# A hybrid encoder layer: order of the in-projection's column groups, who sums and splits x, and what is kept of the weights in DRAM

## The chip, the cores and the metric

The kernel runs on one core of a Trainium2 chip. The core has a matrix engine (TensorE, PE in the profile), a vector engine (VectorE, DVE), a scalar engine (ScalarE, ACT), GpSimd (POOL) and a sync engine (SyncE, SP) that here only issues DMAs; ScalarE and GpSimd can issue DMAs too. Each engine works through its own instructions in order, and semaphores join the engines. The time is microseconds on the device, the median of three runs.

## What is computed

One layer of a streaming encoder, float32, width 1024, for 2048 tokens of a prompt and 8x16 tokens of a decode batch (together 17 tiles of 128 tokens, the last one the decode batch's). In short:

```python
z = x @ w_in                      # 1024 -> 2824 columns
mq, mk, mv, og, li, lf, q, k, v = split_in(z)      # mLSTM: 4 x 512; gates 4 + 4
mlstm = mlstm_chunkwise(mq, mk, mv, li, logsigmoid(lf), C0, n0, m0)   # chunks of 64
attn = band_attend(rope(q), rope(k), v, sinks)     # 8 query, 2 key heads of 64
mix = concat(head_norm(mlstm) * sigmoid(og), attn) @ w_out
x = layer_norm(alpha * x + mix)
up = causal_conv(x @ w_up)                         # 1024 -> 2 x 2816, width 3
x = layer_norm(alpha * x + (silu(gate) * value) @ w_down)
```

The new states, caches and the last rows of the up-projection are outputs as well.

## The kernel before

**Float32 products.** A float32 matrix is split into two fp32r halves: ScalarE copies it to the high half (L205 for weights, L535 for x), VectorE subtracts that to get the low half (L206, L536). A product is then three matmuls: high by high, high by low, low by high.

**Winograd blocks.** The in-projection works on 2x2 blocks with seven products instead of eight, named 1 to 7 (a Strassen-Winograd scheme). Products 1, 2 and 4 use plain blocks of the weights, products 6, 5, 7 and 3 (`SUMS`) use sums of them; likewise with x. The sums of x are t1 to t4 in `x_steps` (L505), made in place in the raw blocks of x by VectorE, which then splits them. For the later token blocks, the low halves of x of products 2, 4 and 5 (b and s in the code at L536) are made by GpSimd, and so are the rope's last adds (L843).

**Tiling.** Four token blocks (`IBLOCKS`) of four tiles, the first with the decode tile besides. For each block five weight groups of 512 columns: two of mLSTM queries and keys, then the mLSTM values (group 2), the output gate (group 3) and the attention's queries (group 4, whose eviction `i_out` at L726 runs through the rope). Each group has seven products of 24 matmuls (`i_product`, L667) that add into three PSUM banks; `i_after` evicts them, on ScalarE and VectorE (L737 to L749). Behind the last products of a block come its direct tiles ("t", `i_direct`, L693): 264 columns of gate logits, attention keys and values, 24 matmuls a tile, in two banks by turns. `i_keys` (L697) evicts them: ScalarE copies gates and values, VectorE makes the rope of the keys (L838, L841, L842), GpSimd adds its two parts (L843), SyncE stores. Then the next block's products 1, 7, 6 and 2 follow.

**The passage.** While a block's last group runs, the next block's x is loaded and its sums and splits are made (`passage`, in `i_dense`): loading behind product 7, then steps 7, 3, b12, t1, t2 behind products 5, 3 and 4, then 1, 6, 2, 5, t4 behind the second direct tile.

**Weights.** `next_raw` (L397) loads 512 KB blocks into raw slots, `next_split` (L436) splits them into a ring of halves, as soon as TensorE has released some. In block 0 `split_first` (L464) makes the sums of the weights from the plain blocks and stores them raw into `zws` in DRAM (L471); the later blocks load the plain blocks from `wi` and the sums from `zws`, and split both again. `d_sums` puts sums of the down-projection's weights into the first groups. The queue of SyncE carries all these transfers in order, and the stores of every output too.

**What is around it.** From block 1 on, the mLSTM and attention work of earlier tiles ("chains") is woven into TensorE's order: that order is written out, the other engines' order comes from the program's order and the scheduler. `logs_of` (gate logarithms of a block) and `i_done` set when a block's chains may begin. The out-projection follows at about 790 us with the rest of the attention, then LayerNorm, then from about 1060 us the feed-forward part: its first block of tokens (`FBLOCKS`) loads six tiles of h from `zh` (L1570), transposes them on TensorE (L1579) and splits them.

## Time and profile before

| | |
|---|---|
| Median of 3 runs | 2517.73 us (2516.81 to 2523.47) |
| Profiled execution | 2523.84 us |
| its span | 2522.1 us |
| mean granted TensorE clock | 0.97 |
| In-projection with its chains | 0 to some 790 us |
| Out-projection | 790 to 1050 us |
| Feed-forward | 1060 us to the end |
| DMA | 600.07 MB, mean 238 GB/s |

How to read the profile's lines: a group of instructions has line, engine, operation, output<-input by the program's names, count, then busy us, the mean of one in ns, the idle time of the engine just before them and what ended most of it. Names: `wraw` raw weights, `w` their halves, `xr` raw x, `oh` and `ol` the halves of x, `dps` the PSUM banks, `u`, `zev` evicted products, `kve` keys and values, `rb` the second part of a rope, `zws` the stored sums of weights, `hst` rows of h. `PE ... <- DVE ...` in a list of waits is TensorE held by VectorE: us in total, how often, the longest. A row of the timeline has start, duration, engine, line, instruction, and in brackets the idle time before it and what ended it. `SPq` is SyncE's queue.

### The profile page before, as it was taken

The numbers are of one execution on the slowest core, as the hardware profiler recorded it, in microseconds if no ns is written. First come the engines' busy times: TensorE is split into PE (matmuls) and PEld (weight loads), VectorE is DVE, ScalarE is ACT, GpSimd is POOL, SyncE is SP. The second block draws the span as 40 slices with busy tenths as digits, with TensorE's granted clock in tenths as the row PEclk, the third lists the DMA queues.
The fourth block names the chain that finished last, engine by engine and source line by source line (L and its number), as shares of the span: only waits on it lengthen the run. The fifth ranks groups of instructions, "written<-read, shape, count | busy, mean of one in ns | idle before, by whom it ended". The sixth has DMA issues, their size and how long they took to land.

```text
span 2522.1 us, 39870 instructions
## 1 busy us (share of the span) xinstructions
PE 2378.4 (94%) x14425; PEld 2176.6 (86%) x14425; DVE 1898.1 (75%) x3221; ACT 1271.8 (50%) x2286; POOL 404.7 (16%) x395
## 2 busy tenths in 40 slices
PE   8989978998997899799999999999999999999998
PEld 7979877987886777589999999999999988778776
DVE  7688497778757776598778877677766678796897
ACT  4444455665564553265555655555545454444453
POOL 0031041223112424310000000001100000220300
PEclk9999989999998999899999999999999999999999
DMA  7858647656756535568776788986998876756652
GB/s 276 296 196 313 215 157 249 220 172 227 240 179 222 187 128 177 203 223 321 291 269 267 255 308 314 314 301 233 316 307 266 263 268 202 245 184 194 219 191 108
DMA packets 290021, 600.07 MB, mean 238 GB/s; under 512 B 46108, under 2 KB 139296, under 8 KB 289824
## 3 DMA queue, kind: packets, MB, share of 16 engines
q1 hardware_dynamic: 288096, 591.23, 68.6%
q0 software_dynamic: 1728, 6.29, 0.7%
q8 instruction: 114, 1.87, 0.3%
q14 instruction: 83, 0.68, 0.1%
HBM read 433.17 MB, written 164.26 MB: 237 GB/s over the span
## 4 chain that ended last, share of the span: by engine, by line
PE 49%; DVE 11%; DMA 4%; issue 4%; ACT 4%; POOL 1%; SPq 0%; DVEq 0%; ACTq 0%; POOLq 0%
PE dps L1714 13%; PE fup L1714 13%; PE fht L1917 5%; PE dps L1917 5%; PE fup L1917 4%; DMA zf<-cc 2%; DVE cc L1762 2%; PE dps L667 2%; PE dps L210 2%; PE dps L211 1%; PE dps L212 1%; ACT cc L1760 1%; DVE uw L206 1%; DVE w L206 1%; ACT sc L1239 1%
## 5 line engine op out<-in xcount | busy, mean ns | idle before, releaser
L1714 PE MATMUL dps<-hh,uw 128*128 128x384 f32 (+1 forms) x1848 | 481.7, 329 | 6.8 <-ACT u L1739 1.9
L1714 PE MATMUL fup<-hh,uw 128*128 128x384 f32 (+1 forms) x1848 | 480.8, 328 | 2.9 <-ACT u L1739 2.3
L1714 PEld LDWEIGHTS dps<-hh,uw 128*128 128x128 f32 x1848 | 330.1, 188 | 10.7 <-ACT u L1739 3.1
L206 DVE TENSOR_TENSOR w<-wraw,w 128x1024 fp32r<-128x1024 f32 (+2 forms) x203 | 262.5, 1301 | 97.3 <-ACT w L205 93.5
L1714 PEld LDWEIGHTS fup<-hh,uw 128*128 128x128 f32 x1848 | 330.3, 188 | 4.8 <-ACT u L1739 3.9
L1762 DVE SCALAR_TENSOR_TENSOR cc<-u,cw,cc 128x768 f32<-128x768 f32 (+1 forms) x264 | 252.4, 977 | 108.7 <-ACT cc L1760 106.9
L205 ACT CAST w<-wraw 128x1024 fp32r<-128x1024 f32 (+2 forms) x203 | 200.5, 995 | 211.9 <-PE dps L667 97.1
L1714 PE MATMUL fup<-hl,uw 128*128 128x384 f32 (+1 forms) x924 | 302.9, 328 | 0.7 <-DVE hl L206 0.7
L1714 PE MATMUL dps<-hl,uw 128*128 128x384 f32 (+1 forms) x924 | 302.5, 327 | 0.0
L667 PE MATMUL dps<-w,oh 128*128 128x256 f32 x1344 | 266.1, 291 | 11.1 <-ACT zev L743 4.4
L667 PEld LDWEIGHTS dps<-w,oh 128*128 128x128 f32 x1344 | 219.0, 195 | 24.1 <-issue 9.2
L205 ACT CAST uw<-wraw 128x1024 fp32r<-128x1024 f32 x126 | 123.0, 978 | 203.8 <-PE dps L1917 94.0
L206 DVE TENSOR_TENSOR uw<-wraw,uw 128x1024 fp32r<-128x1024 f32 x126 | 150.6, 1197 | 61.4 <-ACT uw L205 61.2
L667 PE MATMUL dps<-oh,w 128*128 128x256 f32 x896 | 175.6, 290 | 18.3 <-DVE zev L747 8.7
L667 PE MATMUL dps<-w,ol 128*128 128x256 f32 x672 | 192.1, 286 | 0.0
L1760 ACT ACTIVATE cc<-u,cw 128x768 f32<-128x768 f32 (+1 forms) x132 | 129.6, 998 | 122.1 <-DVE u L1753 60.7
L1917 PE MATMUL fup<-uw,fu 128*128 128x512 f32 x726 | 177.9, 401 | 8.1 <-DVE yacc L1946 4.5
L1917 PEld LDWEIGHTS fup<-uw,fu 128*128 128x128 f32 x726 | 138.2, 191 | 43.5 <-DVE yacc L1946 5.4
L1714 PEld LDWEIGHTS fup<-hl,uw 128*128 128x128 f32 x924 | 173.5, 188 | 1.4 <-DVE hl L206 1.4
L1714 PEld LDWEIGHTS dps<-hl,uw 128*128 128x128 f32 x924 | 173.5, 188 | 0.0
L667 PEld LDWEIGHTS dps<-oh,w 128*128 128x128 f32 x896 | 144.8, 194 | 30.0 <-DVE zev L747 9.8
L1917 PE MATMUL dps<-uw,fu 128*128 128x512 f32 x660 | 164.6, 395 | 0.0
(343 smaller groups left out, 4855.2 us busy)
## 6 DMA issues: line engine op xcount, KB each, us to landing
uw<-zw SPq DMA_DIRECT2D x176, 512.0 KB, 4.7
zw<-uw SPq DMA_DIRECT2D x88, 512.0 KB, 2.9
wv<-wup SPq DMA_DIRECT2D x66, 512.0 KB, 5.3
wraw<-wi SPq DMA_DIRECT2D x65, 512.0 KB, 4.6
wraw<-zws SPq DMA_DIRECT2D x60, 512.0 KB, 3.9
wraw<-zt SPq DMA_DIRECT2D x60, 512.0 KB, 4.2
wraw<-wdn SPq DMA_DIRECT2D x45, 512.0 KB, 4.1
wraw<-wo SPq DMA_DIRECT2D x40, 512.0 KB, 4.4
```

Source lines behind the costliest of these rows:

```text
L205: nc.scalar.copy(hi, src)
L206: nc.vector.tensor_sub(lo, src, hi.bitcast(F32))
L210: mm(out, ah, bh, start=start, stop=False)
L211: mm(out, ah, bl, start=False, stop=False)
L212: mm(out, al, bh, start=False, stop=stop)
L667: mm(o, l, r, start=s in (1, 7) and c == k == i == 0, stop=k == 3 and i == 2, skip_group_check=True)
L1239: nc.scalar.activation(sc[:, j, :N], sc[:, j, :N], AF.Exp, bias=mx[:, j:j + 1], scale=0.125, accum_out=sm[:, j:j + 1])
L1714: mm(ps, l[:, k], r[:, k], start=s in (1, 7) and k == 0 and i == 0, stop=k == 3 and i == 2, skip_group_check=True)
L1760: S.activation(c[:, v], u[:, v, 2:2 + n], AF.Identity, bias=w[3], scale=w[2])
L1762: V.scalar_tensor_tensor(c[:, v], u[:, v, i:i + n], w[i], c[:, v], op0=ALU.mult, op1=ALU.add)
L1917: mm(ps, l[:, k, c], r[:, k], start=s in (1, 4, 7) and u == 0 and k == 0 and i == 0, stop=u == nu - 1 and k == n - 1 and i == 2, skip_grou ...
```

## The change

- The attention's queries are weight group 2 and the mLSTM values group 4; the output gate stays group 3. The last group before the direct tiles so has no rope, and its outputs go to `zv`.
- The sums of x: t3 is made in a buffer of its own (`xt`, a raw slot), t2 adds to it there, t4 goes to the fourth raw block and t1 to the second. The steps are spread over the last group: loading behind product 1, t3 and 7 behind 7, t2 and 6 behind 6, 3 and t4 behind 3, b12 and t1 behind 4; 1 and 2 behind the second direct tile; 4 and 5 behind the fourth. All low halves of x are made by VectorE.
- The rope gets the engine of its last add: VectorE for keys, GpSimd for queries as before.
- Sums of weights of groups 2, 3 and 4 (`KEPT = 2`) are stored into `zws` as two halves after the split in block 0, and in blocks 1 to 3 both halves are loaded straight into the ring of halves: 36 units, with no raw slot and no split. Groups 0 and 1 work as before.
- `logs_of` of a block is called three items (products or tiles) after its second direct tile instead of right behind it, and its chains may begin one item later than before.
- The six tiles of h of the feed-forward's first block are loaded by ScalarE's queue instead of SyncE's.

The diff, with the definition of constants, array allocations and the decode tile's stores cut:

```diff
+KEPT = 2
@@ -95,7 +97,7 @@
     w = f("w_in")[0]
     qa = w[:, 2056:2568].reshape(D, 2, 4, 64).transpose(0, 2, 1, 3).reshape(D, 512)
     qk = [np.concatenate([w[:, c:c + HT], w[:, 512 + c:512 + c + HT]], 1) for c in (0, HT)]
-    wi = np.stack([*qk, w[:, 1024:1536], w[:, 1536:2048], qa], 0)
+    wi = np.stack([*qk, qa, w[:, 1536:2048], w[:, 1024:1536]], 0)
 
     a["wi"] = wi.reshape(NG, 2, 4, P, 2, HT).transpose(0, 4, 1, 3, 2, 5)
     w4 = np.concatenate([w[:, 2052:2056], w[:, 2048:2052], w[:, 2568:2824]], 1)
...
@@ -394,6 +396,10 @@
         while self.next_split() or self.next_raw():
             pass
 
+    def kept(self, u):
+
+        return u[0] == "p" and u[1] > 0 and u[2] >= KEPT and u[3] in SUMS
+
     def next_raw(self):
         nc, a = self.nc, self.a
         if self.ur >= len(self.uq):
@@ -401,7 +407,7 @@
         u = self.uq[self.ur]
 
         there = u[0] == "p" and u[1] == 0 and (u[2] == 0 and u[3] != 1 or u[3] in (5, 4, 3) or u[2:] == (1, 1))
-        if not there and not self.raw_free():
+        if not there and not self.kept(u) and not self.raw_free():
             return False
         self.ur += 1
         if u[0] == "p":
@@ -421,9 +427,11 @@
                     return True
                 self.raw_of[g, quad[s]] = e = self.raw_slot([P, 4, HT])
                 src = a["wi"][g][quad[s]]
+            elif self.kept(u):
+                return True
             else:
                 self.raw_of[u] = e = self.raw_slot([P, 4, HT])
-                src = a["wi"][g][quad[s]] if s in (1, 2, 4) else self.zws[g][SUMS.index(s)]
+                src = a["wi"][g][quad[s]] if s in (1, 2, 4) else self.zws[g][SUMS.index(s)][0]
             nc.sync.dma_start(e[0], src)
         elif u[0] == "g":
             self.raw_of[u] = e = self.raw_slot([P, 2, 264])
@@ -450,7 +458,10 @@
             self.wu[u] = w[:, 0], w[:, 1]
             return True
         hi, lo = self.half([P, 1024]), self.half([P, 1024])
-        if u[0] == "p" and u[1] == 0:
+        if self.kept(u):
+            for i, t in enumerate((hi, lo)):
+                self.nc.sync.dma_start(t.bitcast(F32), self.zws[u[2]][SUMS.index(u[3])][i].rearrange("p a b -> p (a b)"))
+        elif u[0] == "p" and u[1] == 0:
             self.split_first(u[2], u[3], hi, lo)
         else:
             e = self.raw_of.pop(u)
@@ -468,7 +479,8 @@
         a11, a12, a21, a22 = (0, 0), (0, 1), (1, 0), (1, 1)
 
         def keep(q, m):
-            nc.sync.dma_start(self.zws[g][SUMS.index(m)], r[q])
+            if g < KEPT:
+                nc.sync.dma_start(self.zws[g][SUMS.index(m)][0], r[q])
         if s == 7:
             V.tensor_sub(r[a11], r[a11], r[a21])
             keep(a11, 7)
@@ -483,6 +495,9 @@
         for i in range(n):
             c = slice(i * 1024 // n, (i + 1) * 1024 // n)
             self.split(hi[:, c], lo[:, c], f[:, c])
+        if g >= KEPT and s in SUMS:
+            for i, t in enumerate((hi, lo)):
+                nc.sync.dma_start(self.zws[g][SUMS.index(s)][i].rearrange("p a b -> p (a b)"), t.bitcast(F32))
         if s == (6 if g == 0 else 2):
             V.tensor_sub(r[a12], r[a12], r[a11])
             keep(a12, 3)
@@ -505,35 +520,30 @@
 
         nc, V = self.nc, self.nc.vector
         r = lambda q: self.xr[b, q]
-
-        src = {1: 1, 2: 3, 3: 4, "b12": 2, 5: 2, 6: 4, 4: 1}
-        if b == 0:
-            src = {1: 1, 2: 3, 3: 4, "b12": 2, 5: 1, 7: 2, 6: 4, 4: 3}
         for s in steps:
-            if s == "t1":
-                V.tensor_sub(r(src[5]), r(2), r(1))
+            if s == "t3":
+                self.spare = False
+                self.xt = e = self.raw_slot([P, 4, HT]) if b else [self.tp.tile([P, 4, HT], F32, name="xt", tag="qk", bufs=2), False]
+                V.tensor_sub(e[0], r(4), r(2))
             elif s == "t2":
-                V.tensor_sub(r(4), r(4), r(src[5]))
+
+                V.tensor_add(self.xt[0], self.xt[0], r(1))
             elif s == "t4":
-                V.tensor_sub(r(src[4]), r(3), r(4))
-            elif s == "t3":
-                V.tensor_sub(r(2), r(4), r(2))
+
+                V.tensor_sub(r(4), r(3), self.xt[0])
+                self.xt[1] = True
+            elif s == "t1":
+
+                V.tensor_sub(r(2), r(2), r(1))
             else:
-                if s == 7 and b:
-                    e = self.raw_slot([P, 4, HT])
-                    self.spare = False
-                    V.tensor_sub(e[0], r(4), r(2))
-                    e[1] = True
-                    x = e[0]
-                else:
-                    x = r(src[s])
+                x = self.xt[0] if s in (7, 6) else r({1: 1, 2: 3, 3: 4, "b12": 2, 5: 2, 4: 4}[s])
 
                 self.hx[b, s] = h, l = self.x_slot(4 if s == "b12" else s)
                 n = 4 if (b, s) == (0, "b12") else 1
                 for i in range(n):
                     k = slice(i * 4 // n, (i + 1) * 4 // n)
                     nc.scalar.copy(h[:, k], x[:, k])
-                    (nc.gpsimd if b and s in (2, 4, 5) else V).tensor_sub(l[:, k], x[:, k], h[:, k].bitcast(F32))
+                    V.tensor_sub(l[:, k], x[:, k], h[:, k].bitcast(F32))
 
     def x_single(self, *steps):
 
@@ -580,18 +590,20 @@
         self.x_load(0, 3)
         self.x_steps(0, 1)
         self.advance()
-        self.x_steps(0, 2, "t1", "t3", 7, "t2", 6)
+        self.x_steps(0, 2, "t3", 7, "t2", 6)
         self.x_single(4)
-        self.x_steps(0, 5, "t4")
+        self.x_steps(0, "t1", 5, "t4")
         self.sb, self.trans = {}, None
 
-        passage = {7: ["load"], 5: [7], 3: [3], 4: ["b12", "t1", "t2"]}
+        passage = {1: ["load"], 7: ["t3", 7], 6: ["t2", 6], 3: [3, "t4"], 4: ["b12", "t1"]}
         sums = 0
         after = None
         for item in self.items:
             if after:
 
                 after[0] -= 1
+                if after[0] == 1:
+                    self.logs_of(after[1] - 1)
                 if after[0] < 0:
                     self.i_done = after[1]
                     after = None
@@ -607,14 +619,15 @@
                 self.i_keys(b, ti, ps)
                 if ti == 1:
                     if b + 1 < nb:
-                        self.x_steps(b + 1, 1, 6, 2, 5, "t4")
+                        self.x_steps(b + 1, 1, 2)
                     else:
                         self.release(4)
-                    self.logs_of(b)
-                    after = [3, b + 1]
+                    after = [4, b + 1]
                 elif ti == 3 and b or ti == 4:
                     self.release(4)
                     self.x_steps(b, 4)
+                    if b:
+                        self.x_steps(b, 5)
                 self.advance()
                 continue
             _, b, g, s = item
@@ -650,6 +663,7 @@
                 if s == 3:
                     sums += 1
         assert sums == NK2
+        self.logs_of(nb - 1)
         self.chains.hold = False
 
     def i_product(self, b, g, s):
@@ -700,7 +714,7 @@
         nc.scalar.copy(self.gates[b][:, ti, :], ps[:, :8])
         kv = self.mp.tile([P, 2 * P], F32, name="kve", tag="kve", bufs=2)
         nc.scalar.copy(kv[:, P:], ps[:, 136:264])
-        self.rope(ps[:, 8:136], kv[:, :P], t, 1)
+        self.rope(ps[:, 8:136], kv[:, :P], t, 1, nc.vector)
         nc.sync.dma_start(self.zkv[t], kv)
 
     def i_store(self, b, g, i, j, ev):
@@ -711,7 +725,7 @@
             f = 4 * i + 2 * g
             nc.sync.dma_start(self.zqk[b][f:f + 2, :, j * HT:(j + 1) * HT].rearrange("f p m -> p f m"), v)
         else:
-            z = (self.zv, self.zog, self.zqa)[g - 2]
+            z = (self.zqa, self.zog, self.zv)[g - 2]
             for c in range(2):
                 nc.sync.dma_start(z[IBLOCKS[b][2 * j + c]][:, i * HT:(i + 1) * HT], v[:, c])
 
@@ -724,9 +738,9 @@
     def i_out(self, b, g, i, j, src):
 
         nc = self.nc
-        if g == 4:
+        if g == 2:
             A = self.zev()
-            self.rope(src, A, IBLOCKS[b][2 * j], 2)
+            self.rope(src, A, IBLOCKS[b][2 * j], 2, nc.gpsimd)
             self.i_store(b, g, i, j, A)
             return
         ev = src if i else self.zev()
...
@@ -827,7 +841,7 @@
         nc.sync.dma_start(self.zt[0, k], x)
         nc.sync.dma_start(self.zt[1, k], y)
 
-    def rope(self, src, A, t, nt):
+    def rope(self, src, A, t, nt, adder):
 
         V = self.nc.vector
         n = src.shape[-1]
@@ -840,7 +854,7 @@
         over = lambda z: z.to_broadcast([P, nt, n // (64 * nt), 32])
         V.tensor_mul(h(B, 0), h(src, 1), over(ms))
         V.tensor_mul(h(B, 1), h(src, 0), over(sin))
-        self.nc.gpsimd.tensor_add(A, A, B)
+        adder.tensor_add(A, A, B)
 
     def rope_load(self, t, nt):
 
@@ -1567,7 +1581,7 @@
             if ti < len(tiles):
                 tag = tags[ti] if ti < len(tags) else "hst"
                 hs[ti] = fp.tile([P, D], F32, name="hst", tag=tag, bufs=2 if tag == "hst" else 1)
-                nc.sync.dma_start(hs[ti], self.zh[tiles[ti]])
+                (nc.sync if b else nc.scalar).dma_start(hs[ti], self.zh[tiles[ti]])
 
         for ti in range(len(tags)):
             load(ti)
```

More of the change, by code (lines that the diff above doesn't have):

```diff
@@ L289, in setup @@
         self.zqk = [dp.tile([8, P, P * len(b)], F32, name=f"zqk{i}") for i, b in enumerate(IBLOCKS)]
-        self.zws = [[dp.tile([P, 4, HT], F32, name=f"zws{g}_{i}") for i in range(4)] for g in range(NG)]
+        self.zws = [[dp.tile([1 if g < KEPT else 2, P, 4, HT], F32, name=f"zws{g}_{i}") for i in range(4)] for g in range(NG)]
         self.zv = [dp.tile([P, 512], F32, name=f"zv{t}") for t in range(NT)]
@@ L777, in i_batch @@
         t = NPT
-        if g == 4:
+        if g == 2:
             A = self.zev()
-            self.rope(ps, A, t, 1)
+            self.rope(ps, A, t, 1, nc.gpsimd)
             nc.sync.dma_start(self.zqa[t], A)
@@ L793, in i_batch @@
             nc.scalar.copy(ev, ps)
-        nc.sync.dma_start((self.zv, self.zog)[g - 2][t], ev)
+        nc.sync.dma_start((self.zog, self.zv)[g - 3][t], ev)
     def i_transposes(self):
```

## The prediction

> **What bounds the kernel now.** I read the page first, then the span cut into stretches of 100 us, then TensorE's waits, whole and by stretch, and last the timeline where these waits fall.
>
> ```profile
> span 2522.1 us, 39870 instructions
> PE 2378.4 (94%) x14425; PEld 2176.6 (86%) x14425; DVE 1898.1 (75%) x3221; ACT 1271.8 (50%) x2286; POOL 404.7 (16%) x395
> ```
>
> TensorE is the bound, busy for 94% of the span. So the change, which leaves its matmuls as they are, can only take away its gaps and the slow clock behind them. In the stretches the columns are the window, its length, each engine's busy time (with its number of records), the granted clock, the DMA share and GB/s:
>
> ```profile
> 200.00:300.00 100.00, 98.09 (x795) 91.83 (x794) 63.00 (x110) 41.09 (x75) 12.84 (x10) 0.95 0.82 281
> 300.00:400.00 100.00, 80.81 (x617) 74.98 (x615) 83.11 (x210) 51.69 (x128) 31.94 (x21) 0.91 0.56 179
> ```
>
> The first lies inside token block 1 and has almost no gap. The second holds the change of blocks (I call it a passage: the last product of a block, four direct tiles of keys, values and gates at L693, the first products of the next), and 19 us are missing. VectorE, 63 us in the first, has 83 in the second, with more GpSimd beside it. The waits of TensorE over the in-projection say who ends the gaps (us in total, times, longest), and the same question put to the three passages (140 to 215, 335 to 400, 565 to 610 us) and to 1000 to 1120 us gives the second fence:
>
> ```profile
> PE dps L693 <- DVE rb L842: 25.2, 4, 12.1
> PE pq L1185 <- DMA qa<-zqa: 10.2, 1, 10.2
> ...
> PE dps L667 <- DVE zev L747: 8.7, 5, 2.8
> ```
>
> ```profile
> PE dps L693 <- DVE rb L842: 8.6, 1, 8.6
> ...
> PE dps L693 <- DVE rb L842: 12.1, 1, 12.1
> PE ppt L1252 <- DVE C L1173: 3.6, 1, 3.6
> ...
> PE dps L693 <- DVE rb L842: 4.5, 2, 2.7
> PE dps L693 <- DVE u L749: 4.2, 1, 4.2
> ...
> PE fht L1579 <- DMA hst<-zh: 15.3, 1, 15.3
> ```
>
> L842 is the last VectorE instruction of the rope (rotary embedding) on a direct tile's keys: it gives the PSUM bank back, and the third tile needs the first tile's bank. So VectorE's queue in the passage is the bound. The timeline of passage 2 shows what stands in it:
>
> ```profile
> 348.65 0.40 PE L693 MATMUL dps<-w,oh 128*128 128x264 f32 x2
> ...
> 348.85 0.69 DVE L749 TENSOR_TENSOR u<-dps,u 128x512 f32<-128x512 f32 x1 [1.05 <-PE dps L667]
> ...
> 354.37 0.28 PE L693 MATMUL dps<-w,ol 128*128 128x264 f32 x1
> ...
> 359.47 3.35 POOL L536 TENSOR_TENSOR ol<-xr,oh 128x1024 fp32r<-128x1024 f32 x1 [2.26 <-ACT oh L535]
> 360.56 3.36 DVE L206 TENSOR_TENSOR w<-wraw,w 128x1024 fp32r<-128x1024 f32 x1
> 363.84 1.21 DVE L514 TENSOR_TENSOR xr<-xr 128x1024 f32<-128x1024 f32 x1
> ...
> 366.44 0.21 DVE L842 TENSOR_TENSOR rb<-dps,ropet 128x64 f32<-128x64 f32 x1
> ...
> 366.79 0.78 PE L693 MATMUL dps<-w,oh 128*128 128x264 f32 x2 [12.14 <-DVE rb L842]
> ```
>
> From the last product's eviction (348.85) to the rope's end, VectorE works for 17.8 us without a stop, where TensorE has two tiles, 6.0 us, to do (348.65 to 354.65 us). In the queue are the rope of the queries' last output (values are third now, queries last), splits of x and weights, and the Winograd sums t1, t2 (L514, L516). A 128x1024 subtraction takes 1.21 us alone and 3.36 while GpSimd runs its own.
>
> **The change, part by part.** First the passages, where I list VectorE's instructions in the built program between the same two points and take 1.2 us for 128x1024, 0.7 for 128x512, and 0.7 for a tile's rope. The old lengths of passages 1 and 3, and the clock behind each gap:
>
> ```profile
> 163.34 0.68 DVE L749 TENSOR_TENSOR u<-dps,u 128x512 f32<-128x512 f32 x1
> ...
> 175.50 0.21 DVE L842 TENSOR_TENSOR rb<-dps,ropet 128x64 f32<-128x64 f32 x1
> ```
>
> ```profile
> 576.97 0.68 DVE L749 TENSOR_TENSOR u<-dps,u 128x512 f32<-128x512 f32 x1
> ...
> 584.80 0.21 DVE L842 TENSOR_TENSOR rb<-dps,ropet 128x64 f32<-128x64 f32 x1
> ```
>
> ```profile
> 175.00:190.00 15.00, 11.24 (x64) 11.09 (x65) 13.54 (x32) 4.66 (x9) 9.49 (x6) 0.73 0.45 147
> ...
> 366.00:375.00 9.00, 8.21 (x47) 8.24 (x48) 8.40 (x22) 2.89 (x7) 5.20 (x4) 0.65 0.47 149
> ...
> 583.00:600.00 17.00, 12.47 (x84) 11.03 (x84) 13.35 (x24) 7.76 (x15) 10.60 (x6) 0.87 0.48 159
> ```
>
> - Passage 1, 12.4 us before. Left are u, t4, a split of x, one of weights, t1, a rope: 0.7+4x1.2+0.7 = 6.2 us, against 7.1 us of TensorE (two tiles as in passage 2, and 12 matmuls of the sample tile at 0.12, 98.09/795). The 8.6 us go. The clock lost up to 0.27x15 = 4 us; I take 3 of them. -11.5.
> - Passage 2, 17.8 before. Left are u, small instructions of the attention, three of 128x512 of the mLSTM chain, a split of x, t1, one of weights, a rope: 9.4 with some stretch, against 5.7 from 348.85 on. The wait falls from 12.1 to 3.7 (between 2 without stretch and 6 with more), and of the 0.35x9 = 3.2 us of clock 2.5 go. The 3.6 us of C (attention) stay. -11.
> - Passage 3, 8.0 before. Left are u, two splits, t1, a rope: 5.0 against 5.7. The 4.5 go, of the 4.2 for u (splits stand ahead of it in both programs) half, and 1.5 of 0.13x17 = 2.2 us of clock. -8.
>
> Here a rule weighs on one term. The Trainium skill, "TensorE: Matmul & The Clock Gate", Part 1, says that one idle window of about 3.4 us brings the half clock. By it the 3.7 us left in passage 2 would keep the clock's loss, and the sum below would be 2.5 us smaller; the gaps quoted, all longer than that, agree.
>
> Next, the work inside the blocks:
>
> ```profile
> L206 DVE TENSOR_TENSOR w<-wraw,w 128x1024 fp32r<-128x1024 f32 (+2 forms) x184 | 235.7, 1289 | 84.8 <-ACT w L205 81.0 <-PE pk L1187 1.6 <-DMA og<-zog 1.2
> L205 ACT CAST w<-wraw 128x1024 fp32r<-128x1024 f32 (+2 forms) x184 | 180.6, 990 | 191.9 <-PE dps L667 97.1 <-PE psx L677 16.9 <-DVE wraw L478 14.8
> ...
> L536 DVE TENSOR_TENSOR ol<-xr,oh 128x1024 fp32r<-128x1024 f32 (+1 forms) x23 | 30.2, 1331 | 3.1 <-ACT oh L535 3.1
> L536 POOL TENSOR_TENSOR ol<-xr,oh 128x1024 fp32r<-128x1024 f32 x9 | 26.5, 2951 | 12.4 <-ACT oh L535 8.6 <-DVE w L206 3.8
> L843 POOL TENSOR_TENSOR kve<-kve,rb 128x128 f32<-128x128 f32 x17 | 16.3, 959 | 46.6 <-DVE rb L842 34.1 <-issue 5.6 <-DVE gl L965 3.1
> L838 DVE TENSOR_TENSOR kve<-dps,ropet 128x128 f32<-128x128 f32 x16 | 4.5, 280 | 1.7 <-ACT kve L702 1.7
> ```
>
> 36 weight splits go (4 sums, 3 groups, blocks 1 to 3): VectorE -36x1.289 = -46.4, ScalarE -36x0.990 = -35.6. VectorE takes GpSimd's nine splits of x (9x1.331 = 12.0) and 17 adds of keys (no row has this add; 0.28 by the multiplication of the same shape, between 0.21 of the 128x64 rope step and 0.96 of GpSimd's: 3.6 to 16; I take 4.8, as VectorE did the like shape). Net -29.6 for VectorE. GpSimd loses 26.5+16.3 = 42.8 us. TensorE's waits in the blocks, the 8.7 us for zev among them, shrink with a VectorE that is 5% lighter there: nothing at worst, 10 at best, I take -5. Queries third puts their ropes (17 on GpSimd's 128x512 add) where TensorE has 39 to 49 matmuls, some 5 us at 0.12, before it needs the bank: cost nothing, under the cover of these.
>
> The transfers:
>
> ```profile
> uw<-zw SPq DMA_DIRECT2D x176, 512.0 KB, 4.7
> ...
> wraw<-zws SPq DMA_DIRECT2D x60, 512.0 KB, 3.9
> ```
>
> ```profile
> 225.00:275.00 50.00, 49.63 (x417) 46.63 (x417) 31.69 (x58) 21.40 (x38) 6.98 (x7) 0.98 0.94 332
> ...
> 255.00:265.00 10.00, 9.63 (x99) 9.27 (x99) 6.01 (x13) 6.18 (x15) 1.15 (x1) 1.00 1.04 392
> ```
>
> 72 loads of halves take the place of 36 raw ones, and 24 stores of 12: 48x0.524 = +25 MB. A half may only be loaded when TensorE has let go of its buffer, and from then 82 to 144 matmuls (10 to 18 us) remain to its use; a pair lands in about 4.7 to 9.4 us (the first row is the same kind of load, later in this kernel). So it is hidden, unless the DMA is full: 225 to 275 us has a share of 0.94. Four units of one group bring 2.1 MB more there, 6.3 us at 332 GB/s. Over three blocks the cost is 0 to 19; I take +4, since other stretches have room (a share of 0.56 in 300 to 400 us). SP's queue is in order, and a load that waits for TensorE holds up the raw loads and the stores behind it; the same lead covers them. The chains start one product later: 0 to 24x0.12 = 2.9 us a block; I take +1.5 in all.
>
> A rule speaks against this part: "DMA: Bandwidth & Descriptors", section "Bandwidth", of the Trainium skill gives some 358 GB/s as the limit of HBM for a core. By it 332+42 GB/s would not fit and 2 us a block would be lost, 6 where I have 4; the row with 392 GB/s goes against that limit here.
>
> The attention after the in-projection finds its queries loaded early, but its keys (kva) are issued in the same place, behind the same backlog, so of the 10.2 us I take -1.5. The rows of h:
>
> ```profile
> 1055.03 5.55 POOL L1462 TENSOR_TENSOR ymix<-ymix,o_ln_b 128x1024 f32<-128x1024 f32 x2 [2.29 <-DVE ymix L1461]
> ```
>
> ```profile
> 1062.21 2.96 SPq L1570 DMA_DIRECT2D hst<-zh x6
> ```
>
> ScalarE's queue need not wait for SP's earlier issues, but the first row's buffer is still given free by that GpSimd add, which ends at 1060.6: 1.6 us before 1062.21. -1.5 of 15.3.
>
> The sum: -11.5-11-8-5-1.5-1.5+4+1.5 = -33. The profiled execution took 2523.84 us, so 2490.8 on its scale. It lies 6.1 above the median of the runs, 2517.73; from that, 2485.
>
> **The rivals.**
> - The passages gain half. For it: GpSimd keeps the attention's adds, which stretch VectorE in passage 2, and ends of waits often uncover another (C, u). Against: passages 1 and 3 come out below TensorE's own time. -15 for the passages, -3 in blocks, -1.5 at h, +4.5: -15, 2503.
> - The halves come late, and it is slower. Place: each of the 36 kept units, in SP's in-order queue behind a wait for TensorE. For it: the share of 0.94 and the loss of the raw slots' head start. Against: 10 to 18 us of lead for 5 to 9 us of landing. At 2 us a unit +72-36 = +36, 2554; it decides from about 1 us a unit on.
> - The change doesn't move the bound: the queries' ropes, on one rb buffer and GpSimd's add, hold up banks inside the blocks, 12 evictions x 1.3 us = 15, on top of the first rival: about 0, 2518. For it, GpSimd's 128x512 add is as slow as before. Against, the 5 us of cover.
> - More goes: the rest of the blocks' waits too (-10), passage 2 whole (-4 more), the queries' 10.2 us (-8 more): about -50, 2468. For it, VectorE and GpSimd are lighter everywhere.
>
> **How the numbers follow.** Forecast 0.50, half 0.18, late halves 0.11, not moved 0.07, more 0.14. Within 0.3% (7.6 us, about what a measurement of this kernel can tell) lies the one not moved. Faster 0.82, same 0.07, slower 0.11. The range runs from the last rival to beyond the first, with the bounds of the transfers (+15) on the forecast inside it: 2465 to 2512.
>
> **What would show it.** The waits on the rope's last step in the passages gone in 1 and 3 and near 4 us in 2; 300 to 400 us of TensorE at about 92; GpSimd some 43 us lighter, VectorE some 30. No wait of L667's matmuls on a DMA of halves, and the h wait at about 14. Waits on DMA of halves in blocks 1 to 3, or on rb in their middle, would make it wrong.

## The result and the profile after

The changed kernel takes 2476.26 us (median of four runs, 2474.47 to 2482.57), the kernel before beside it 2518.85: a ratio of 0.9833, 95% interval 0.9811 to 0.9855. That is 42.6 us less, where 33 were forecast. The profiled executions stand 47.9 us apart (2523.84 and 2475.97). Line numbers of the changed kernel are 14 higher in the in-projection (L693 is now L707, L842 is L856, L667 is L681), 10 higher for the splits of x (L536 is L546), and 2 higher for those of weights (L206 is L208).

The first lines of the changed kernel's page:

```profile
span 2473.9 us, 39844 instructions
PE 2358.5 (95%) x14425; PEld 2160.9 (87%) x14425; DVE 1838.3 (74%) x3211; ACT 1240.5 (50%) x2250; POOL 361.8 (15%) x369
...
DMA packets 296932, 625.23 MB, mean 253 GB/s; under 512 B 46876, under 2 KB 140064, under 8 KB 296736
```

GpSimd is 42.9 us lighter, VectorE 59.8, and the DMA moves 25 MB more. TensorE's waits over the in-projection, then those of 140 to 215, 335 to 400, 540 to 600 and 1000 to 1120 us:

```profile
PE dps L707 <- DVE rb L856: 7.5, 3, 5.0
PE dps L681 <- ACT zev L757: 6.7, 3, 3.0
...
PE dps L681 <- DVE zev L761: 5.7, 6, 2.2
PE dps L681 <- ACT dps L785: 5.1, 3, 3.5
...
PE pscs L1404 <- DMA kvc<-kcT: 4.2, 1, 4.2
PE pk L1201 <- DMA kva<-zkv: 3.7, 1, 3.7
```

```profile
PE pgr L991 <- DVE g L982: 2.9, 1, 2.9
PE dps L681 <- DVE rb L856: 2.8, 1, 2.8
PE dps L707 <- DVE rb L856: 0.8, 1, 0.8
...
PE dps L707 <- DVE rb L856: 5.0, 1, 5.0
PE ppt L1266 <- DVE C L1187: 1.3, 1, 1.3
...
PE dps L707 <- DVE rb L856: 1.7, 1, 1.7
...
PE fht L1593 <- DMA cw<-cw: 14.3, 1, 14.3
```

The third tile's wait for the rope in the passages was 8.6, 12.1 and 4.5 us and is 0.8, 5.0 and 1.7. The 10.2 us for the queries at the out-projection are gone, and 3.7 us for the keys stand there. The line "cw<-cw" is taken for the wait for the rows of h (the profile names a small load issued 0.4 us behind the first of them); it is 1 us shorter. New is the wait for kvc, the decode tile's cached keys, and longer is the one for L785, a bank's copy by ScalarE (L771 before, 1.8 us). Right behind passages 1 and 3 the next products (L681) wait 2.8 and 1.5 us for the rope of the last direct tile.

Where the time came from is best seen by cutting the span at the first and the last matmul of each block's direct tiles. In the changed kernel they are at 159.25 and 171.96, 342.74 and 360.87, 551.01 and 564.90, 739.74 and 745.54 us; in the kernel before at 160.21 and 184.01, 348.65 and 375.05, 570.39 and 595.30, 775.00 and 782.28. A "passage" here runs from the first to the last of the four direct tiles. All in us:

| | block 0 | passage 1 | block 1 | passage 2 | block 2 | passage 3 | block 3 | last tiles | to the transposes of h |
|---|---|---|---|---|---|---|---|---|---|
| before | 160.2 | 23.8 | 164.6 | 26.4 | 195.3 | 24.9 | 179.7 | 7.3 | 284.4 |
| after | 159.2 | 12.7 | 170.8 | 18.1 | 190.1 | 13.9 | 174.8 | 5.8 | 274.1 |
| difference | -1.0 | -11.1 | +6.1 | -8.3 | -5.2 | -11.0 | -4.9 | -1.5 | -10.3 |

The sum is -47.0 (the differences are of the unrounded times). The feed-forward part from the first up-projection matmul on, at 1092.7 us before and 1044.4 after, has the same 1429 us.

In the middle of passage 2, VectorE's rows and TensorE's wait are now these:

```profile
342.94 0.69 DVE L763 TENSOR_TENSOR u<-dps,u 128x512 f32<-128x512 f32 x1 [0.27 <-PE dps L681]
...
345.87 0.39 DVE L1254 TENSOR_TENSOR asm<-asm,aes 128x4 f32<-128x4 f32 x1 [1.69 <-ACT sc L1253]
...
353.34 0.21 DVE L856 TENSOR_TENSOR rb<-dps,ropet 128x64 f32<-128x64 f32 x1
...
353.69 0.78 PE L707 MATMUL dps<-w,oh 128*128 128x264 f32 x2 [4.96 <-DVE rb L856]
```

### The profile page after: what moved, and what is told of

The parts are those of the page before. It is cut to its first block, busy times and chain, and to the rows that moved or that the text cites. A ratio compares the mean times of both kernels' runs of the same rounds, so it can differ in the third digit from the quotient of the medians.

```text
span 2473.9 us, 39844 instructions
## 1 busy us (share of the span) xinstructions
PE 2358.5 (95%) x14425; PEld 2160.9 (87%) x14425; DVE 1838.3 (74%) x3211; ACT 1240.5 (50%) x2250; POOL 361.8 (15%) x369
## 4 chain that ended last, share of the span: by engine, by line
PE 64%; DVE 10%; DMA 6%; issue 3%; ACT 3%; POOL 2%; SPq 0%; DVEq 0%; ACTq 0%; POOLq 0%
PE dps L1728 17%; PE fup L1728 17%; PE dps L681 7%; PE fht L1931 5%; PE dps L1931 5%; PE fup L1931 3%; PE dps L212 1%; PE dps L213 1%; PE dps L214 1%; DVE w L208 1%; PE ppo L1272 1%; DVE uw L208 1%; ACT sc L1253 1%; PE ppt L1266 1%; DMA txy<-wdn 1%
## 5 line engine op out<-in xcount | busy, mean ns | idle before, releaser
L681 PE MATMUL dps<-w,oh 128*128 128x256 f32 x1344 | 263.0, 290 | 12.0 <-ACT zev L757 6.7
L208 DVE TENSOR_TENSOR w<-wraw,w 128x1024 fp32r<-128x1024 f32 (+2 forms) x167 | 206.2, 1244 | 61.4 <-ACT w L207 54.6
L207 ACT CAST w<-wraw 128x1024 fp32r<-128x1024 f32 (+2 forms) x167 | 162.9, 984 | 156.4 <-PE dps L681 74.1
L681 PEld LDWEIGHTS dps<-w,oh 128*128 128x128 f32 x1344 | 217.0, 193 | 24.9 <-issue 8.1
L208 DVE TENSOR_TENSOR uw<-wraw,uw 128x1024 fp32r<-128x1024 f32 x126 | 150.7, 1197 | 61.6 <-ACT uw L207 61.4
L681 PE MATMUL dps<-w,ol 128*128 128x256 f32 x672 | 191.2, 285 | 0.0
L681 PE MATMUL dps<-oh,w 128*128 128x256 f32 x896 | 176.4, 291 | 13.8 <-DVE zev L761 5.7
L681 PEld LDWEIGHTS dps<-oh,w 128*128 128x128 f32 x896 | 145.4, 194 | 24.2 <-DVE zev L761 6.9
L1931 PE MATMUL dps<-uw,fu 128*128 128x512 f32 x660 | 164.7, 395 | 0.0
```

Of the source, the lines that this page charges most:

```text
L207: nc.scalar.copy(hi, src)
L208: nc.vector.tensor_sub(lo, src, hi.bitcast(F32))
L681: mm(o, l, r, start=s in (1, 7) and c == k == i == 0, stop=k == 3 and i == 2, skip_group_check=True)
L1931: mm(ps, l[:, k, c], r[:, k], start=s in (1, 4, 7) and u == 0 and k == 0 and i == 0, stop=u == nu - 1 and k == n - 1 and i == 2, skip_grou ...
```

## The experiments

Each kernel was timed in five rounds beside the kernel before; ratios are to it, with 95% intervals. The table shows the same cuts for them, from one profiled execution of each. Behind the transposes of h these executions have 1453 to 1459 us, and the runs of one kernel lie up to 13 us apart, so a few us between two medians or two cuts say little by themselves.

| kernel | median us | ratio | block 0 | pass. 1 | block 1 | pass. 2 | block 2 | pass. 3 | block 3 | to h |
|---|---|---|---|---|---|---|---|---|---|---|
| changed kernel, again (e1) | 2477.96 | 0.9838 (0.9812-0.9865) | 159.4 | 12.9 | 170.2 | 18.2 | 189.3 | 15.8 | 173.2 | 275.2 |
| no halves (e2) | 2496.83 | 0.9905 (0.9884-0.9926) | 158.8 | 11.5 | 181.4 | 19.9 | 192.0 | 13.5 | 178.8 | 277.8 |
| queries last (e3) | 2497.44 | 0.9911 (0.9885-0.9936) | 155.0 | 19.8 | 173.3 | 20.7 | 188.0 | 19.5 | 174.3 | 276.3 |
| old sums (e4) | 2478.77 | 0.9835 (0.9812-0.9859) | 160.1 | 11.5 | 164.9 | 20.2 | 188.2 | 13.1 | 176.6 | 276.6 |
| before + order (e5) | 2497.96 | 0.9909 (0.9891-0.9926) | 166.0 | 13.2 | 163.1 | 20.6 | 195.4 | 13.7 | 184.6 | 276.0 |
| before + halves (e6) | 2517.45 | 0.9990 (0.9978-1.0001) | 159.9 | 23.7 | 163.3 | 25.4 | 191.4 | 23.5 | 178.6 | 283.4 |
| before + both (e7) | 2489.73 | 0.9881 (0.9861-0.9901) | 164.7 | 13.2 | 164.3 | 19.9 | 195.3 | 12.9 | 178.4 | 277.8 |
| x on GpSimd (e8) | 2489.28 | 0.9874 (0.9853-0.9895) | 159.9 | 14.1 | 173.2 | 19.3 | 191.5 | 15.7 | 180.3 | 275.1 |
| all halves (e9) | 2488.39 | 0.9873 (0.9859-0.9886) | 163.3 | 13.3 | 191.5 | 17.5 | 185.3 | 12.5 | 168.0 | 274.3 |
| keys on GpSimd (e10) | 2485.76 | 0.9864 (0.9850-0.9877) | 169.5 | 11.6 | 173.8 | 18.2 | 191.0 | 12.6 | 174.6 | 275.7 |
| h by SyncE (e11) | 2480.22 | 0.9848 (0.9831-0.9866) | 156.7 | 13.1 | 170.1 | 18.1 | 188.2 | 15.3 | 172.8 | 277.6 |
| cache by ScalarE (e12) | 2471.26 | 0.9807 (0.9789-0.9825) | 159.2 | 12.9 | 165.0 | 18.6 | 187.6 | 13.5 | 175.2 | 277.3 |

**The yardstick.** 

> The changed kernel once more, as the yardstick of this series, which takes parts of it back one at a time: 2476 us, ratio to the kernel before 0.983. Both theories (the time was won in the passages by a shorter VectorE queue; or by less splitting work everywhere) expect this alike.

2477.96 us, ratio 0.9838. The cuts come back within some 1 us of the first profile but for passage 3 and block 3 (about 2). "More" below is against this median. The intervals of x on GpSimd, all halves and keys on GpSimd touch the yardstick's; against the mean of all eight runs of the changed kernel in the two series, 2478.6, their means are 10.1, 9.7 and 7.4 us longer.

**No halves.**

```diff
-KEPT = 2
+KEPT = 5
```

> The changed kernel with the sums of weights of all groups stored raw and split again in every block (KEPT = 5). VectorE has 46 us more of weight splits and ScalarE 36, the DMA 25 MB less. Theory A (the passages' queue did it, the halves are a small gain less their transfers): +4 us, 2480, and the direct tiles' waits in passage 2 about 1 to 2 us longer. Rival B (the lighter VectorE did it): +20 us or more. Rival C (the halves' transfers cost more than the splits): 2 to 6 us faster than the changed kernel, and the 4.2 us wait for the cache of keys in block 1 gone.

2496.83 us, 19 more than the changed kernel: B by its size. Of C one sign comes, since TensorE no longer waits for the cache of keys in block 1, but that doesn't pay for the splits. The loss is inside the blocks (block 1 +11, blocks 2 and 3 together +8), not in the passages. Block 1 of this kernel, then of the yardstick:

```profile
170.28:351.70 181.42, 164.55 (x1255) 154.77 (x1254) 123.70 (x278) 75.64 (x153) 27.07 (x19) 0.91 0.71 230
```

```profile
172.28:342.48 170.20, 156.43 (x1256) 147.44 (x1255) 109.53 (x266) 63.42 (x141) 24.24 (x19) 0.94 0.86 293
```

TensorE's own waits are 17 us for 14; the other 8 us are the same matmuls at a lower granted clock (0.91 for 0.94). The halves' term was sized far too small in the prediction. The edit gives work back to VectorE and to ScalarE alike, and changes the use of the raw slots and the loads, so this run doesn't show that it is VectorE alone.

**Queries last.**

```diff
-    wi = np.stack([*qk, qa, w[:, 1536:2048], w[:, 1024:1536]], 0)
+    wi = np.stack([*qk, w[:, 1024:1536], w[:, 1536:2048], qa], 0)
...
-        if g == 2:
+        if g == 4:
```

(and the outputs' arrays with it.) 

> The changed kernel with the weight groups in the old order (values third, queries last). Theory A: the rope of the last output is back in each passage (1.5 to 2.6 us of VectorE), so 2 to 3 us a passage, and the queries' wait at the start of the out-projection is back (some 7 us): +14 us, 2490. Rival B (the passage's length is set by sums and splits alone): only the 7 us at the out-projection, 2483. Rival C (the order is what emptied the passages): +30 us, 2506.

2497.44 us, 19.5 more: between A (14) and C (30). The passages take +6.9, +2.5 and +3.7 us. A wait of 8.5 us for the queries is back at the out-projection, and yet the stretch to the transposes is only 1 us longer than in the yardstick. With the old order the other edits still take 15 us off the passages of the kernel before (60 us for 75).

**Old sums.**

```diff
-        passage = {1: ["load"], 7: ["t3", 7], 6: ["t2", 6], 3: [3, "t4"], 4: ["b12", "t1"]}
+        passage = {7: ["load"], 5: [7], 3: [3], 4: ["b12", "t1", "t2"]}
...
-                        self.x_steps(b + 1, 1, 2)
+                        self.x_steps(b + 1, 1, 6, 2, 5, "t4")
...
-                    if b:
-                        self.x_steps(b, 5)
```

(with the old in-place sums.) 

> The changed kernel with the old sums of x and their old places (t1 and t2 behind the last product, steps 1, 6, 2, 5, t4 behind the second direct tile), all low halves still on VectorE. Theory A: two splits and one sum (3.6 us) more between the last product and the third direct tile in each passage, and more splits behind it: the three passages lose 4 to 6 us each and their clock: +15 us, 2491. Rival B (VectorE's total counts, not its place): no change, within 4 us, since the number of instructions is the same.

2478.77 us against 2477.96: B. Of the passages only the second is longer, by 2 us; block 3 is 3 us longer, and block 1 is 5 us shorter. That last gain comes from another place: the cached keys, for which TensorE waits 4.1 us in the yardstick, were here issued before a store that holds the queue, and the wait is gone:

```profile
264.12 0.33 SPq L1395 DMA_DIRECT2D kvc<-kcT  x1
```

So the fair comparison is with e12 below, which lacks that wait too: up to the transposes of h it takes 1015.1 us, this kernel 1016.9. (The rest of the difference of these two executions lies in the feed-forward part, which neither edit touches.) The spreading of the sums, the part with the most code, is worth some 2 us at most by these cuts, and nothing in the median. (A kernel with the old sums and the cache in the other queue was not run.)

**The order alone**, on the kernel before:

```diff
-    wi = np.stack([*qk, w[:, 1024:1536], w[:, 1536:2048], qa], 0)
+    wi = np.stack([*qk, qa, w[:, 1536:2048], w[:, 1024:1536]], 0)
...
-        if g == 4:
+        if g == 2:
```

> The kernel before with only the weight groups in the new order (queries third, values last). Taking the order back cost the changed kernel some 19 us. Theory A (the parts add up): -19 us, 2501, each passage 3 to 7 us shorter. Rival B (without the lighter VectorE the freed place is filled by the splits waiting there): -8 us or less, 2512, and the passages hardly shorter.

2497.96 us, 23.7 less than the kernel before: more than A, with passages shorter by 10.6, 5.8 and 11.2 us, as short as in the changed kernel but for passage 2. Blocks 0 and 3 lose 6 and 5 of it, and the stretch to h gains 8. VectorE's timeline in passage 2 of this kernel shows how one rope of the queries can be worth so much:

```profile
342.50 0.69 DVE L749 TENSOR_TENSOR u<-dps,u 128x512 f32<-128x512 f32 x1 [0.39 <-PE dps L667]
...
344.00 1.26 DVE L536 TENSOR_TENSOR ol<-xr,oh 128x1024 fp32r<-128x1024 f32 x1 [0.21 <-ACT oh L535]
...
346.38 1.22 DVE L206 TENSOR_TENSOR w<-wraw,w 128x1024 fp32r<-128x1024 f32 x1
347.51 1.22 DVE L536 TENSOR_TENSOR ol<-xr,oh 128x1024 fp32r<-128x1024 f32 x1
348.65 1.22 DVE L206 TENSOR_TENSOR w<-wraw,w 128x1024 fp32r<-128x1024 f32 x1
349.78 1.22 DVE L514 TENSOR_TENSOR xr<-xr 128x1024 f32<-128x1024 f32 x1
...
351.12 3.17 DVE L516 TENSOR_TENSOR xr<-xr 128x1024 f32<-128x1024 f32 x1
...
354.35 0.21 DVE L842 TENSOR_TENSOR rb<-dps,ropet 128x64 f32<-128x64 f32 x1
```

From u to the rope's end it is 12.1 us, 17.8 before, though all the splits and sums that stood there before still do. The kernel before had these rows in the same place (start, duration):

```profile
349.58 1.77 DVE L838 TENSOR_TENSOR zev<-u,ropet 128x512 f32<-128x512 f32 x1
...
353.09 1.92 POOL L1242 TENSOR_TENSOR sc<-sc,asm 128x1024 f32<-128x1024 f32 x1 [0.59 <-DVE asm L1241]
...
353.78 2.31 DVE L536 TENSOR_TENSOR ol<-xr,oh 128x1024 fp32r<-128x1024 f32 x1
...
354.98 2.24 POOL L843 TENSOR_TENSOR zev<-zev,rb 128x512 f32<-128x512 f32 x1
...
356.02 2.28 DVE L206 TENSOR_TENSOR w<-wraw,w 128x1024 fp32r<-128x1024 f32 x1
```

The rope itself took 2.6 us (1.77, 0.41, 0.39). The rest is stretch: a split of x (2.31 for 1.26), and splits of weights (2.28 and 3.36 for 1.22), which fell beside GpSimd's instructions and now do not. GpSimd's two splits of x, 6.13 us from 350.39 on in the order-alone kernel, still stretch one sum to 3.17.

**The halves alone**, on the kernel before (the change's edits of `next_raw`, `next_split`, `split_first` and `zws`):

```diff
+        if self.kept(u):
+            for i, t in enumerate((hi, lo)):
+                self.nc.sync.dma_start(t.bitcast(F32), self.zws[u[2]][SUMS.index(u[3])][i].rearrange("p a b -> p (a b)"))
```

> The kernel before with only the split sums of groups 2 to 4 kept as halves. Taking them back cost the changed kernel some 19 us, most of it inside the blocks. Theory A (the parts add up): -19 us, 2501, blocks 1 to 3 together 15 us shorter, passages alike. Rival B (in the old order the queries' rope and its place in the last group still hold VectorE, so the lighter VectorE can't be used): -8 us or less.

2517.45 us, ratio 0.9990 with an interval that holds 1: B. The passages stay, and blocks 1 to 3 give 1 to 4 us each by the cuts, which flatter it: its profiled execution, 2513.48 us, is the shortest of its twelve, and that of the kernel before, 2523.84, lies above all of its first runs (2516.81 to 2523.47). The same 36 units that are worth 19 us in the changed kernel are worth some 4 in the old one, if anything. VectorE is busy for 38 us less here (1860.0), so that alone doesn't buy time. The reason that B gives, the queries' rope in the last group, is not tested further.

**Order and halves**, on the kernel before:

> The kernel before with both, the new order and the halves, but with its old sums of x, x's low halves of products 2, 4, 5 and the keys' adds on GpSimd, the chains' old start and h on SyncE's queue. Theory A (order and halves are the whole gain): -38 us, 2482, within 4 us of the changed kernel. Rival B (the work taken from GpSimd is needed too, since its instructions stretch VectorE's beside them): 2490 or above, with waits of 3 us and more left in the passages.

2489.73 us: A is out, and B holds at its edge, though a wait of more than 3 us for the rope is left in passage 2 alone (6.4 us; 1.4 and 1.2 in the others). The two are worth 32 us together, and 12 are missing to the changed kernel. In the cuts they are missing in blocks 0, 2 and 3 (about 5 us each) and at h, not in the passages; block 1 is even 6 us shorter, where the wait for the cached keys is 0.8 us instead of 4.1.

**x on GpSimd.**

```diff
-                    V.tensor_sub(l[:, k], x[:, k], h[:, k].bitcast(F32))
+                    (nc.gpsimd if b and s in (2, 4, 5) else V).tensor_sub(l[:, k], x[:, k], h[:, k].bitcast(F32))
```

> The changed kernel with the nine low halves of x of products 2, 4 and 5 back on GpSimd (3 us each there, 1.2 us on VectorE). Theory A (they stretch VectorE's instructions beside them and come late): +5 us, 2482, with the passages 2 to 3 us longer each. Rival B (VectorE, lighter by 12 us, gains as much): within 2 us. Rival C (VectorE's total decides): -4 us.

2489.28 us, 11.3 more: A's direction at twice its size, and C is out. But the place that A named is wrong: the passages take 1 us at most, and blocks 1 to 3 take 3, 2 and 7. In block 1 the wait for the cached keys grows by as much (from 4.1 us), and in block 3 there is a wait for gate logarithms right behind the passage, which the yardstick doesn't have:

```profile
PE pscs L1404 <- DMA kvc<-kcT: 7.2, 1, 7.2
```

```profile
PE dps L681 <- DVE gl L979: 5.4, 1, 5.4
```

Here is VectorE of this kernel:

```profile
PE 2362.6 (95%) x14425; PEld 2164.2 (87%) x14425; DVE 1849.9 (74%) x3202; ACT 1239.3 (50%) x2250; POOL 381.2 (15%) x378
```

With nine instructions fewer than the changed kernel, VectorE is busy for 11.6 us more. The nine subtractions take 22.7 us on GpSimd; nine of them at 1.22 us are 11 us on VectorE. So by this estimate VectorE's other instructions are together some 22.6 us longer, as much as GpSimd is busy with the nine. Taking them off GpSimd made VectorE's own instructions shorter by more than the work that it took over.

**All halves.**

```diff
-KEPT = 2
+KEPT = 0
```

> The changed kernel with the sums of all five groups kept as halves (KEPT = 0): 24 more units are not split again (VectorE 31 us less, ScalarE 24 less), at 17 MB more of DMA, in the first groups where the sums of the down-projection's weights are loaded too. Theory A (the lighter VectorE goes on paying): -5 to -10 us, 2470, blocks 1 to 3 shorter. Rival B (the DMA, at a share of 0.87 and 0.88 in 100 to 300 us of the changed kernel, is full there): +3 us or more, with waits on DMA in the blocks.

2488.39 us, 10.4 more. A's gain comes in blocks 2 and 3 (4 and 5 us), B's loss with waits on DMA in block 1 (21 us), and block 0 loses 4. The waits of block 1 (176 to 368 us) of this kernel, and the stretch of 200 to 300 us:

```profile
PE pq L1199 <- DMA qa<-zqa: 9.7, 1, 9.7
PE pscs L1404 <- DMA kvc<-kcT: 8.0, 1, 8.0
```

```profile
200.00:300.00 100.00, 79.29 (x608) 74.00 (x606) 44.96 (x95) 20.29 (x42) 17.64 (x12) 0.87 0.88 317
```

No wait is for a half itself: late are the attention's loads. But the DMA share is the 0.88 of the changed kernel, with 317 GB/s for 305, so a full DMA doesn't explain it alone; e12 asks for the queue, in the changed kernel.

**Keys on GpSimd.**

```diff
-        self.rope(ps[:, 8:136], kv[:, :P], t, 1, nc.vector)
+        self.rope(ps[:, 8:136], kv[:, :P], t, 1, nc.gpsimd)
```

> The changed kernel with the 17 adds of the keys' rope back on GpSimd (0.96 us each there). Theory A (its rb buffer is held longer, and the next tile's rope waits): +1 to +4 us, 2480, block 0 up to 2 us later. Rival B (5 us less on VectorE): -2 to 0.

2485.76 us, 7.8 more, beyond A's range; block 0 alone takes 10 us more, though only three of the 17 adds fall into it. Its waits (0 to 169 us) have 5.3 us for splits of weights on VectorE, 0.9 in the changed kernel, and the timeline shows the way there:

```profile
33.80 4.97 POOL L857 TENSOR_TENSOR kve<-kve,rb 128x128 f32<-128x128 f32 x1 [10.86 <-DVE rb L856]
...
38.79 0.35 SPq L718 DMA_DIRECT2D zkv<-kve  x1
...
39.66 0.44 SPq L830 DMA_DIRECT2D txy<-wdn  x1
...
43.38 0.69 DVE L836 TENSOR_TENSOR txy<-txy 128x512 f32<-128x512 f32 x1 [4.59 <-DMA txy<-wdn]
...
46.40 0.80 PE L681 MATMUL dps<-oh,w 128*128 128x256 f32 x2 [4.49 <-DVE w L208]
```

GpSimd takes 4.97 us for the third add, beside VectorE's splits. The store of these keys holds SyncE's queue until the add is done (the DMA share is 0.14 from 30 to 40 us, 0.87 in the yardstick). The load behind it comes late, VectorE stands 4.6 us for it with splits of weights waiting behind, and TensorE 4.5 us for such a split. Block 1 has the wait for the cached keys at 7.2 us again. So it is not A's buffer that costs the time. On VectorE the add takes 0.28 us, as estimated.

**h by SyncE.**

```diff
-                (nc.sync if b else nc.scalar).dma_start(hs[ti], self.zh[tiles[ti]])
+                nc.sync.dma_start(hs[ti], self.zh[tiles[ti]])
```

> The changed kernel with the six tiles of h loaded by SyncE's queue again. Theory A (the buffer is given free by GpSimd's last add, the queue gives 1 to 2 us): +1.5 us, 2479, the wait of the transposes near 15.5 us instead of 14.3. Rival B (nothing): the wait stays.

2480.22 us, 2 more, within the runs' spread; the wait is 15.3 us, and 14.3 in the changed kernel: A as far as the profile goes. The rows of the changed kernel:

```profile
1009.00 5.55 POOL L1476 TENSOR_TENSOR ymix<-ymix,o_ln_b 128x1024 f32<-128x1024 f32 x2 [2.29 <-DVE ymix L1475]
...
1014.57 6.92 ACTq L1584 DMA_DIRECT2D hst<-zh  x6
```

The loads start when GpSimd's add ends (1014.55), as foreseen.

**The cache by ScalarE.** In the changed kernel TensorE waits until 275.50 us, and the loads it waits for are here, in SyncE's queue:

```profile
261.34 0.89 SPq L463 DMA_DIRECT2D w<-zws  x2
266.33 0.80 SPq L730 DMA_DIRECT2D zqa<-zev  x2
...
267.72 0.40 SPq L463 DMA_DIRECT2D w<-zws  x1
268.51 0.80 SPq L730 DMA_DIRECT2D zqa<-zev  x2
269.40 0.44 SPq L463 DMA_DIRECT2D w<-zws  x1
269.89 0.50 SPq L1392 DMA_DIRECT2D kvc<-kcT  x1
```

The queue stands from 262.2 to 266.3 at a store of queries, which are in the middle of the block now and end with GpSimd's add (2.21 us from 264.10 on).

```diff
-            nc.sync.dma_start(kc, a["kcT"][:, bs])
-            nc.sync.dma_start(vc, a["vc"][:, bs])
+            nc.scalar.dma_start(kc, a["kcT"][:, bs])
+            nc.scalar.dma_start(vc, a["vc"][:, bs])
```

> The changed kernel with the four loads of the decode tile's cached keys and values (kvc, L1392 and L1393) in ScalarE's queue instead of SyncE's. In the changed kernel TensorE waits 4.2 us for the second pair in block 1, since the loads stand in SyncE's queue behind loads of halves and stores of queries that wait for other engines. Theory A (the order of SyncE's queue makes them late): that wait goes, block 1 is 4 to 8 us shorter with the clock behind it, 2471. Rival B (the DMA engines are full there, at a share of 0.87 in 252 to 272 us): the wait stays and the time is 2477.

2471.26 us, block 1 5 to 6 us shorter. The same place there:

```profile
263.70 0.33 ACTq L1392 DMA_DIRECT2D kvc<-kcT  x1
```

```profile
272.00:292.00 20.00, 20.00 (x179) 18.64 (x180) 8.61 (x17) 7.79 (x19) 1.19 (x2) 0.95 0.75 262
```

The load is issued 6 us earlier, TensorE does not wait for it (in the changed kernel this window has 16.50 us of TensorE at a clock of 0.76), and the DMA engines carry 333 GB/s from 252 to 272 us where they carried 295. So the queue made it late: A. This is the fastest of all kernels; its interval (0.9789 to 0.9825) and the yardstick's (0.9812 to 0.9865) overlap. But four of its five runs lie below all eight of the changed kernel (whose shortest is 2474.47), and the wait and the cut of block 1 fit.

## Why the prediction was right, point by point

- **The passages**, -30.5 forecast, -30.4 in the cuts (-11.1, -8.3, -11.0 for -11.5, -11 and -8). The mechanism, VectorE's queue ahead of the third tile's bank, holds: in passage 2 it is 10.6 us long (u at 342.94, the rope's end at 353.55) for 9.4 forecast, and the wait 5.0 for 3.7. VectorE itself stands for some 2.6 us of the 10.6, for ScalarE (1.69 in the row shown), and a list of its instructions doesn't have that. Behind this wait the granted clock is 0.54 from 353.7 to 357 us and 1.00 after it, so some 1.5 us are lost where it was 3.2; I had let 0.7 stay. But that the sum agrees so closely is partly luck, since the list credited the wrong edits. The order alone gives 27.6 of the 30 us, the other edits without it 15 (e3), so the two overlap; with both there, the old sums take nothing back. The rope and the stretch beside GpSimd were the length in passage 2, not t1, t2 and the splits. I had set the whole list against TensorE's two tiles, without asking of each edit by itself how much of it they would have covered anyway. And the gaps that I quoted for the clock are not all longer than 3.4 us: behind one of 2.7 us, which ended at 591.03 us in the kernel before, the clock was 0.61 from 591 to 595 us.
- **Inside the blocks**, -5 for the lighter VectorE, and +5.5 for transfers and the later chains: +0.5 forecast, -6.4 in the cuts, last tiles included. The term for the lighter VectorE was mis-sized: taking the halves away alone costs 19 us. Its size hangs on the other edits, since on the old kernel it is some 4 at most. The order goes the other way, 23.7 alone and 19.5 taken back. Taken back one by one, halves, order, splits of x and adds of keys cost 19, 19.5, 11 and 8 us, more than the whole 42.6, so these prices can't be added. The later start of the chains has no run of its own.
- **GpSimd's work moved to VectorE** stood in the sum as a cost to VectorE of 16.8 us within the -29.6. VectorE lost 59.8. By the busy times of e2, e8 and e10 the halves took 49 us off it, close to the 46.4 forecast, but the moved splits took off 11.6 and the moved adds 2.1, where 16.8 were to come on. The stretch of 1.21 to 3.36 us, which the prediction quoted for the passage, was not carried into the rest. In time e8 and e10 put the two moves at 11 and 8 us; how much of that is the stretch itself is open, since 3 us of each is the wait for the cached keys, and the 10 us of block 0 in e10 come through SyncE's queue.
- **The transfers**, +4: no half is ever waited for, as the lead of 82 to 144 matmuls said. A price is paid by another load in SyncE's queue: the 4.2 us for kvc and its slow clock, 5 to 6 us in block 1 (e12). How much of it the halves make is open: without them (e2) the wait is gone, but with them it is none in e4, 0.8 us in e7 and 7.2 in e8 and e10, as the load happens to stand before or behind the queries' store at which the queue stops. The prediction named what is queued behind and called it covered; that was wrong for loads that have no slack of their own.
- **Queries in the middle**, nothing forecast: 5.1 us of waiting for L785 in three places, where it was 1.8 before. ScalarE's copy waits for the rope's last read of the bank. The rival had priced it at 15.
- **The out-projection's start**, -1.5 forecast; the wait fell from 10.2 to 3.7, and the stretch to h by 10.3 with 1 us of it at h. The wait for the queries is gone whole, and the keys come earlier than I took. But with queries last (e3) the wait is 8.5 us and the stretch still 276.3, so it isn't the wait alone. All kernels with the new order or the later chains have 274 to 278 us here, the two with neither 283 and 284. Which of the chain's places makes that is open.
- **h**, -1.5 forecast, -1.0 by the wait.
- **The sum** is so 10 us short in the median, by the blocks and the out-projection, which both gave more than their terms. Of the signs, GpSimd's 42.9 us, h's 14.3 and the 5.0 in passage 2 came; VectorE is lighter by twice the 30, and TensorE has 88.8 us in 300 to 400 us instead of 92.

## What to carry to other kernels

Price a change of engine for an instruction by what it does to its neighbours: nine subtractions on GpSimd cost VectorE some 22 us here, and doing them itself 11. Before crediting an edit in a queue, ask how much of the queue the waiting engine covers anyway, and do one part alone: here the reordering was about half of the gain and the elaborate rescheduling next to none. When loads are added to an in-order queue, look for the loads without slack that will stand behind them, and give those another queue. And before an edit is given its price, look whether the time was lost where the edit works: three of these experiments (e4, e8, e10) moved block 1 by 3 to 5 us, and with it went the wait for one load that none of them touched.

## What the runs showed of the hardware

VectorE's 128x1024 subtraction takes 1.21 to 1.22 us alone and 2.3 to 3.4 beside GpSimd's tensor instructions; GpSimd's 128x128 add, 0.46 us at its shortest in block 0 of e10, took 4.97 beside VectorE's. With GpSimd's nine splits on VectorE, VectorE's own busy time fell by 11.6 us (1849.9 to 1838.3). One core drew 371 GB/s over 20 us (232 to 252 us of e12), and in the whole of block 1 (171 to 343 us) of that kernel no load kept TensorE waiting for more than 0.2 us:

```profile
232.00:252.00 20.00, 18.95 (x153) 17.94 (x153) 10.43 (x24) 6.53 (x12) 3.96 (x3) 1.00 1.00 371
```

The Trainium skill ("DMA: Bandwidth & Descriptors", section "Bandwidth") gives some 358 GB/s as the limit of HBM for a core, and says that a core gets about that when both cores on the memory stream; this run, on one core, lies above it. Six loads of 512 KB take 6.92 us to issue in ScalarE's queue and 3.05 in SyncE's (e11, the row below), so the other queue saved 1.0 us for a start that came 1.6 us earlier behind the add.

```profile
1013.11 3.05 SPq L1584 DMA_DIRECT2D hst<-zh  x6
```
